# One hybrid decoder block on one core: no remainders on GpSimd, row tiles by token halves, another order of the products of the merge, and accumulating transfers

## The chip, the core and the metric

The kernel runs on one NeuronCore of a Trainium2 chip. The core has a matrix engine (TensorE, PE in the profile; PEld is its loading of weights), a vector engine (VectorE, DVE), an activation engine (ScalarE, ACT), a programmable vector engine (GpSimd, POOL) and an engine that issues most transfers (SyncE, SP). Each works through its own queue in order and waits on semaphores. Matrix products land in PSUM, eight banks of 128 partitions by 512 floats; everything else works on SBUF, 128 partitions wide. The metric is the device time of one execution in microseconds. The kernel before takes 2135.2 us, the median of three runs (2126.42 to 2137.53).

## The reference

One layer, batch 1, 1024 tokens, model width 1024, all in float32. What is computed:

```
h      = rms_norm(x, norm_mix_g) * (1 + scale) + shift        # scale, shift, gate from c @ w_ada
proj   = h @ w_in                                             # q, k, v of two mixers, gates
ya     = rms_norm(diff_attention(q1, q2, k1, k2, v))          # 8 heads, causal, 128 wide values
ym     = sigmoid(mo) * rms_norm(mlstm_chunkwise(q, k, v))     # 4 heads, 256 wide
merged = sigmoid(ga) * (ya @ w_a) + sigmoid(gm) * (ym @ w_m)
x      = x + gate * (merged @ w_out)
x      = x + gate' * (relu(h' @ w_ff1)^2 @ w_ff2)             # h' from x as h above
```

The change touches the way operands are split (everywhere), the product ya @ w_a with the merge behind it, the product merged @ w_out, and the first groups of w_ff1.

## The kernel before

**Split operands.** PE multiplies in a reduced format (F32R). Every float32 operand v is split into a high part (a copy on ACT into F32R) and a remainder v - high (a subtraction), and a product of two operands is three matmuls: high x high, high x remainder, remainder x high. The copy is line 319 in `parts` and line 152 in `load_w`; the subtraction is `split_lo`, line 138. `split_lo` and `parts` take an argument `pool`: True puts the subtraction on GpSimd, False on DVE, None lets a running count choose (`pick`, which charges GpSimd three units where DVE has one, or a plain alternation within `split_lo`). `add` (line 315) and `sub` (line 312) choose in the same way.

**Seven products instead of eight.** The large products are done in 2x2 blocks of 512 by the Strassen-Winograd scheme: sums of blocks are formed on both sides, seven products are made, and sums of the products give the four output blocks. Class `Chunks` does it for ya @ w_a, for merged @ w_out and for w_ff2. `prep` forms the next product's operand sums (`operands`) and splits them, in two halves q; `run` issues a product, four blocks j of 12 matmuls each (line 327, tiles `cps`, `s_op`, `t_op`), and calls an `out` function after each block, `out_a` for w_a and `out_o` for w_out. The operand tiles exist twice (`self.s`, `self.t`), so that `prep` runs one product ahead, and its splits wait until the product two before has been read. The orders are `ORDER_X` = (1, 7, 2, 4, 5, 6, 3) for w_a (and w_ff2) and `ORDER_Y` = (1, 2, 5, 6, 3, 7, 4) for w_out. In `out_a`, product 6 adds into three tiles and merges two blocks.

**The merge.** `merge` takes a finished block of ya @ w_a, in PSUM or SBUF. It loads the same block of the other branch (`mb`, from mb_d in DRAM, line 1677) and of the gate (`sga_d`), makes tanh on ACT (line 1285), the gating (sg + 1) * block on DVE (line 1288) and the addition of mb on DVE (line 315). mb_d is written before by `m_unit` through transfers that GpSimd issues (line 1302).

**Stages.** After the norm and the first projections come the mLSTM heads, with the gate projections (`gate_unit`) woven in between; the attention heads, each with the next head's projection (`at_qk`); in the last head the reload of ym (`reload`) and the units of ym @ w_m; then w_a, w_out, and the feed-forward. Weights are loaded ahead by `plan`, whose entries call `load_w`. Before the feed-forward, `half0` and `right` form and split the row blocks of h' for the first four groups, on GpSimd or DVE as `pick` says.

**Row tiles.** `ActX` holds split rows for hT and later ym in four tiles of the pool `xp`, which has four slots. They are cut by halves of the features: tile [r][k // 4] holds all 1024 tokens of four of the eight feature blocks, for r = high or remainder. The tiles of the merge (`mg`) and one operand set of `Chunks` take the same four slots afterwards.

**Order of the work.** The program is written out as a sequence of calls. The framework then lists it for each engine by itself: it takes ready work in program order by its own estimates of durations, and an operation whose inputs are there early can be placed ahead of its place in the program.

Of the kernel before, what the change touches and what calls it, by code (L numbers as in the profile page):

```python
# [17 lines left out]
P = 128  # L18
# [18 lines left out]
def kernel(  # L37
# [131 lines left out]
    class ActX:  # L169


        def __init__(self, name):
            self.t = [[xp.tile([P, 4, S], F32R, name=f"{name}{r}{i}", tag="x") for i in range(2)] for r in range(2)]

        def at(self, k, t0, n):
            return tuple(self.t[r][k // 4][:, k % 4, t0:t0 + n] for r in range(2))
# [350 lines left out]
    def modulate(q):  # L527
# [15 lines left out]
        def step(n):  # L543
# [9 lines left out]
            hh, hl = (hT.t[r][q][:, k:k + 2, m * 256:(m + 1) * 256] for r in range(2))  # L553
# [205 lines left out]
    class Conv(Group):  # L759
# [9 lines left out]
        def out(self, t, hf, n, a, b, into):  # L769
            c = crow[t][:, hf * 512:hf * 512 + 512]  # L770
            if b is None:
                nc.scalar.activation(c, a, AF.Copy)
            else:
                add(c, a, b, None if (t, hf) == (1, 1) else False)
            if (t, hf) in ((0, 1), (1, 0)):
                behind.extend(self.conv(t))
# [25 lines left out]
    class Gate(Group):  # L802
# [9 lines left out]
        def out(self, t, hf, n, a, b, into):  # L812
# [5 lines left out]
            else:  # L818
                add(c, a, b, None if (t, hf) == (1, 1) else False)
# [39 lines left out]
    def ml_in(h, hd):  # L859


        def half(hf):
# [7 lines left out]
            for i in (1, 0):  # L870
                for t in range(2):
                    d = hd["qk"][i, t, hf] = wt("r", [P, 2, 512], "qk", F32R)
                    parts((d[:, 0, :], d[:, 1, :]), hd["kc"][t][:, ts_] if i else q[:, t, :])

        def vals(g):
# [7 lines left out]
            parts((vt[:, :, 0, 0:256], vt[:, :, 1, 0:256]), vr)  # L883
# [212 lines left out]
    def at_v(h, vts):  # L1096
# [3 lines left out]
        def read(g):  # L1100
# [3 lines left out]
            parts((vt[:, :, 0, :], vt[:, :, 1, :]), vr.rearrange("p t (a d) -> p (t a) d", a=2))  # L1104
# [212 lines left out]
    def gate_cols(i):  # L1317
        cols((C_GA, C_GM)[i // 4] + (i % 4) * 256, True)

    def qk_cols(h):  # L1320
# [3 lines left out]
        plan.append(lambda: load_w([(srcs[q], lambda v, q=q: v[:, :, q * P:(q + 1) * P]) for q in range(2)], KT, True))  # L1324
# [6 lines left out]
    for h in range(AH):  # L1331
        if h % 2 == 0 and h // 2 not in (0, 1, 2):
            cols(C_AV + h * P, True)
# [4 lines left out]
    for u in range(4):  # L1338
        plan.append(lambda u=u: load_cols(w_m[0], u * 256, True))
# [142 lines left out]
    for h in range(AH):  # L1482
# [18 lines left out]
    class Chunks:  # L1501
# [6 lines left out]
        def __init__(self, xs):  # L1508
            self.n, self.jobs, self.made, self.tmp = 0, [], 0, {}
# [15 lines left out]
        def add(self, order, left, right, out, sums=None):  # L1525
            self.jobs += [(i, order, left, right, out, sums) for i in order]
# [9 lines left out]
        def prep(self):  # L1536
# [5 lines left out]
            i, order, left, right, _, sums = self.jobs[n]  # L1542
            s, t = self.s[n % 2], self.t[n % 2]
            for q in range(2):
                l, r = self.operands(i, order[1] == 7, left, right, sums, q)
                self.split(s(q), l)
                self.split(t(q), r)

        def operands(self, i, x, left, right, sums, q):
            b11, b12, b21, b22 = (right.get((m, q)) for m in (11, 12, 21, 22))  # L1550
            if sums is None:
                a11, a12, a21, a22 = (left[m, q] for m in (11, 12, 21, 22))
            two = range(2)

            def tmp(tag, name):
                return [wt(tag, [P, 512], name) for _ in two]
# [4 lines left out]
            r = {1: b11, 2: b21, 3: b22, 4: b21, 5: b12, 6: b11, 7: b12}[i]  # L1561
            if x:
                if i == 7:
                    r = tmp("f", "t3")
                    for k in two:
# [5 lines left out]
            elif i == 5:  # L1571
                r = self.tmp["r", q] = tmp("f", "t1")
                for k in two:
                    sub(r[k], b12[:, k], b11[:, k], False)
            elif i == 6:
                minus(b12, b22, b12)
                for k, v in enumerate(self.tmp["r", q]):
                    sub(b11[:, k], b22[:, k], v, False)
            elif i == 4:
                minus(b21, b21, b11)  # L1580
            if sums is not None:
                return sums(i, q), r
            l = {1: a11, 2: a12, 3: a12, 4: a22, 5: a21, 6: a11, 7: a21}[i]
            if i == 3:
                minus(a12, a12, a11)
            elif x:
                if i == 7:
                    l = tmp("m", "s3")
                    for k in two:
                        sub(l[k], a11[:, k], a21[:, k], False)  # L1590
                elif i == 5:
                    add(a21, a21, a22, False, 2)
                elif i == 6:
                    minus(a11, a21, a11)
            elif i == 5:
                l = self.tmp["l", q] = tmp("m", "s1")
                for k in two:
                    add(l[k], a21[:, k], a22[:, k], False)
            elif i == 6:
                minus(a21, a11, a21)  # L1600
                for k, v in enumerate(self.tmp["l", q]):
                    sub(a11[:, k], v, a11[:, k], False)
            return l, r

        def run(self):

            i, order, _, _, out, _ = self.jobs[self.n]
# [21 lines left out]
    ORDER_Y = (1, 2, 5, 6, 3, 7, 4)  # L1629
# [44 lines left out]
    def merge(dst, c, f0, t0):  # L1674

        mb = wt("m", [P, 512], "mb")
        nc.sync.dma_start(mb, mb_d[f0:f0 + P, t0:t0 + 512])
        sg = gated(sga_d, f0, t0)(c)
        busy(1)
        add(dst, sg, mb, False)  # L1680

    def out_a(i, j, ps):
        f0, f1 = j * P, 512 + j * P
        if i == 1:
            nc.scalar.activation(u1[:, j], ps, AF.Copy)
        elif i == 7:
            nc.scalar.activation(m22[:, j], ps, AF.Copy)
        elif i == 2:
            merge(m11[:, j], ps, f0, 0)
        elif i == 4:  # L1690
            add(m12[:, j], ps, u1[:, j], False)
        elif i == 5:
            add(m22[:, j], ps, m22[:, j], False)
            add(m22[:, j], m22[:, j], u1[:, j], False)
        elif i == 6:
# [384 lines left out]
```

## Time and profile before

| | before |
|---|---|
| median of three runs | 2135.2 us (2126.42 to 2137.53) |
| the profiled execution's own time | 2137.04 us |
| its span, first to last instruction | 2135.2 us |
| busy: PE, DVE, ACT, POOL | 2001.3, 1660.5, 1045.5, 234.0 us |
| granted PE clock over the span | 0.97 |
| POOL's subtractions of 128x1024 | 36, 2453 ns each |
| transfers on the queue of POOL | 9.44 MB, against 285.35 MB on SP's |

Busy time is the union of an engine's instructions; the idle time of an engine is put down to what ended it, by semaphore. A row of a group reads: line, engine, operation, output and input tiles, shapes, count, then busy time and mean duration in ns, then the idle time of the engine before them and its releasers. A row of a timeline reads: start, length, engine, line, operation, tiles, shape, count, and in brackets the idle time just before. Where operations of DVE follow each other closely, the recorded durations overlap by some 0.08 us, so their spacing is shorter than their duration.

### The profile page before, as it was taken

How to read it: one execution, taken by the hardware profiler on the slowest of the kernel's cores; microseconds unless marked ns; L12 is line 12 of the kernel's file. 1: busy time of each engine (PE TensorE's matmuls, PEld its weight loads, DVE VectorE, ACT ScalarE, POOL GpSimd, SP SyncE). 2: the span in 40 equal slices, each digit the busy share in tenths (PEclk: the TensorE clock that was granted, in tenths of full speed). 3: DMA queues.
4: the chain of work that ended last, by engine and by line, in shares of the span. 5: the costliest groups of instructions: out<-in, count | busy, mean ns of one | idle time of the engine just before them, and what ended most of it. 6: DMA issues, size and time to landing. Idle time of an engine off the chain costs nothing. (4 is left out here: it accounts for less than half of the span.)

```text
span 2135.2 us, 30324 instructions
## 1 busy us (share of the span) xinstructions
PE 2001.3 (94%) x11201; PEld 1732.3 (81%) x11201; DVE 1660.5 (78%) x2887; ACT 1045.5 (49%) x1966; POOL 234.0 (11%) x251
## 2 busy tenths in 40 slices
PE   5889999999889999999999999888799999899999
PEld 5889898888778899898988788677678888788887
DVE  7876668987765468989877747998777667898896
ACT  5522234444565557777756634435444555433332
POOL 0000000002232211111112410004400000000000
PEclk7999999999999999999999999999899999999999
DMA  8354453235655342222222665503344445845432
GB/s 284 111 163 156 150 162 118 91 107 193 192 177 162 107 122 60 80 60 80 60 66 69 202 222 169 171 1 123 114 169 156 153 148 201 305 139 167 150 117 80
DMA packets 210634, 296.72 MB, mean 139 GB/s; under 512 B 14067, under 2 KB 132494, under 8 KB 210486
## 3 DMA queue, kind: packets, MB, share of 16 engines
q1 hardware_dynamic: 207542, 285.35, 41.8%
q0 software_dynamic: 2944, 9.44, 1.2%
q8 instruction: 88, 1.44, 0.3%
q14 instruction: 60, 0.49, 0.1%
HBM read 206.43 MB, written 79.93 MB: 134 GB/s over the span
## 5 line engine op out<-in xcount | busy, mean ns | idle before, releaser
L327 PE MATMUL cps<-t_op,s_op 128*128 128x512 f32 x2016 | 478.4, 398 | 27.3 <-ACT s_op L319 10.9
L327 PEld LDWEIGHTS cps<-t_op,s_op 128*128 128x128 f32 x2016 | 383.1, 191 | 119.6 <-ACT s_op L319 12.6
L319 ACT ACTIVATE w_op<-w_st 128x512 fp32r<-128x512 f32 (+1 forms) x192 | 130.6, 695 | 183.8 <-PE pb L327 57.8
L138 DVE TENSOR_TENSOR w_op<-w_st,w_op 128x512 fp32r<-128x512 f32 (+1 forms) x192 | 146.7, 784 | 6.3 <-ACT w_op L319 4.1
L165 PE MATMUL ps<-w_hi,hT 128*128 128x256 f32 x512 | 146.9, 287 | 0.0
L166 PE MATMUL ps<-w_lo,hT 128*128 128x256 f32 x512 | 146.7, 286 | 0.0
L167 PE MATMUL ps<-w_hi,hT 128*128 128x256 f32 x512 | 146.2, 286 | 0.0
L319 ACT ACTIVATE s_op<-act 128x1024 fp32r<-128x1024 f32 x56 | 58.4, 1051 | 142.9 <-PE cps L327 108.0
L138 POOL TENSOR_TENSOR w_lo<-w_st,w_hi 128x1024 fp32r<-128x1024 f32 x36 | 87.9, 2453 | 313.3 <-ACT w_hi L152 310.0
L1198 ACT ACTIVATE ee<-ee,mneg 128x256 f32<-128x256 f32 (+7 forms) x128 | 98.4, 770 | 21.0 <-DVE mneg L1194 20.6
L327 PE MATMUL pa<-b,w_op 128*128 128x512 f32 x384 | 96.4, 402 | 6.7 <-ACT m L430 6.6
L1188 PE MATMUL lg<-kb,qe 128*128 128x512 f32 (+3 forms) x384 | 96.1, 361 | 4.2 <-DVE kb L1160 1.9
L327 PE MATMUL pc<-bt,w_op 128*128 128x512 f32 x384 | 96.1, 396 | 3.8 <-DVE w_op L138 2.0
L166 PEld LDWEIGHTS ps<-w_lo,hT 128*128 128x128 f32 x512 | 98.0, 191 | 1.5 <-issue 0.9
L165 PEld LDWEIGHTS ps<-w_hi,hT 128*128 128x128 f32 x512 | 97.9, 191 | 0.8
L167 PEld LDWEIGHTS ps<-w_hi,hT 128*128 128x128 f32 x512 | 98.0, 191 | 0.2
L327 PEld LDWEIGHTS pa<-b,w_op 128*128 128x128 f32 x384 | 74.1, 194 | 23.1 <-ACT m L430 7.6
L327 PEld LDWEIGHTS pc<-bt,w_op 128*128 128x128 f32 x384 | 71.1, 188 | 24.6 <-DVE w_op L138 7.0
L315 DVE TENSOR_TENSOR acc<-cps,acc 128x512 f32<-128x512 f32 x116 | 76.9, 684 | 13.0 <-PE cps L327 12.8
L715 DVE SCALAR_TENSOR_TENSOR ac<-crow,cond,ac 128x256 f32<-128x256 f32 x112 | 54.0, 482 | 34.2 <-DMA crow<-in_w_ada_dram 32.5
L1194 DVE CUSTOM_DVE_ANT_0 ee<-lg,bs 128x512 f32<-128x512 f32 (+4 forms) x128 | 70.1, 559 | 12.4 <-PE lg L1188 11.4
L138 DVE TENSOR_TENSOR s_op<-act,s_op 128x1024 fp32r<-128x1024 f32 x56 | 68.2, 1219 | 5.4 <-ACT s_op L319 5.3
(418 smaller groups left out, 4948.8 us busy)
## 6 DMA issues: line engine op xcount, KB each, us to landing
w_st<-in_w_in_dram SPq DMA_DIRECT2D x72, 512.0 KB, 4.5
act<-act_d SPq DMA_DIRECT2D x56, 512.0 KB, 3.6
w_st<-in_w_ff_dram SPq DMA_DIRECT2D x36, 512.0 KB, 4.1
crow<-in_w_ada_dram SPq DMA_DIRECT2D x32, 512.0 KB, 3.9
w<-in_w_ff_dram SPq DMA_DIRECT2D x32, 512.0 KB, 5.0
act_d<-s SPq DMA_DIRECT2D x48, 256.0 KB, 2.0
wa<-in_w_ada_dram SPq DMA_DIRECT2D x16, 512.0 KB, 4.8
mq_d<-cv SPq DMA_DIRECT2D x16, 512.0 KB, 2.8
```

The lines of the kernel that those rows point to most:

```text
L138: return (nc.gpsimd if pool else nc.vector).tensor_tensor(dst, src, hi.bitcast(F32), op=ALU.subtract)
L165: nc.tensor.matmul(o, lhsT=ah, rhs=bh, start=first, stop=False)
L166: nc.tensor.matmul(o, lhsT=ah, rhs=bl, start=False, stop=False)
L167: nc.tensor.matmul(o, lhsT=al, rhs=bh, start=False, stop=last)
L315: (nc.gpsimd if pick(pool, n) else nc.vector).tensor_tensor(o, a, b, op=ALU.add)
L319: nc.scalar.activation(dst[0], src, AF.Copy)
L327: nc.tensor.matmul(ps, lhsT=p, rhs=q, start=first and k == 0 and r == 0, stop=k == 3 and r == 2, skip_group_check=True,)
L715: nc.vector.scalar_tensor_tensor(ac, stv[:, k, :], cond[:, kk:kk + 1], ac, op0=ALU.mult, op1=ALU.add)
L1188: nc.tensor.matmul(lg[:, 0:max(256, w)], lhsT=hd["q"][hf][e][:, r, q4 * P:(q4 + 1) * P], rhs=hd["k"][e][:, c0:c0 + max(256, w)], start=r = ...
L1194: nc.vector.tensor_tensor_reduce(ee[:, c0:c0 + w], lg[:, 0:w], hd["bs"][:, n - c0 - w:n - c0][:, ::-1], -0.125, first, ALU.add, ALU.min, last,
L1198: nc.scalar.activation(ee[:, 0:n], ee[:, 0:n], AF.Exp, bias=mneg[:, e:e + 1], scale=-1.0, accum_out=ssum[:, e:e + 1])
```

## The change

1. Every remainder and every block sum that was on GpSimd, or could be by `pick`, goes to DVE: `parts(..., False)`, `sub(..., False)`, and False in the weight loads of `plan` and in `reload`. GpSimd keeps the powers of the norms, masks, memsets and its transfers.
2. `ActX` is cut by halves of the tokens: tile [t0 // 512][r] holds all eight feature blocks of 512 tokens.
3. In `Chunks.operands`, products 6 and 7 without given sums use another form of the scheme: product 6 forms all operand sums, half of them (`rest`) behind its own splits, and product 7 takes a22 minus the changed a11. The orders are `ORDER_Y` = (1, 2, 6, 7, 4, 5, 3) for w_a and `ORDER_Z` = (1, 2, 6, 5, 3, 7, 4) for w_out. w_ff2 keeps `ORDER_X`. `out_a` and `out_o` follow: product 6 now adds into one tile. w_out's weights are loaded in the order 11, 21, 12, 22.
4. `merge` gates into the destination itself, and a transfer issued by GpSimd adds mb_d's block to it in SBUF (`accum_op=ALU.add`).

```diff
-            self.t = [[xp.tile([P, 4, S], F32R, name=f"{name}{r}{i}", tag="x") for i in range(2)] for r in range(2)]
+            self.t = [[xp.tile([P, KT, 512], F32R, name=f"{name}{r}{i}", tag="x") for r in range(2)] for i in range(2)]
...
-                    parts((d[:, 0, :], d[:, 1, :]), hd["kc"][t][:, ts_] if i else q[:, t, :])
+                    parts((d[:, 0, :], d[:, 1, :]), hd["kc"][t][:, ts_] if i else q[:, t, :], False)
...
-        cols((C_GA, C_GM)[i // 4] + (i % 4) * 256, True)
+        cols((C_GA, C_GM)[i // 4] + (i % 4) * 256, False)
...
-        plan.append(lambda u=u: load_cols(w_m[0], u * 256, True))
+        plan.append(lambda u=u: load_cols(w_m[0], u * 256, False))
...
-            filler += reload(ym, ym_d, True) + units[0:12 * 2]
+            filler += reload(ym, ym_d, False) + units[0:12 * 2]
...
+            l = {1: a11, 2: a12, 3: a12, 4: a22, 5: a21, 6: a11, 7: a11}[i]
+            r = {1: b11, 2: b21, 3: b22, 4: b21, 5: b12, 7: b11}.get(i)
+            behind = ()
+            if i == 6:
+                add(a21, a21, a22, False, 2)
+                minus(a11, a21, a11)
+                minus(b12, b12, b11)
+                r = [wt("f", [P, 512], "t2") for _ in range(2)]
+                for k in range(2):
+                    sub(r[k], b22[:, k], b12[:, k], False)
+                def rest():
+                    for k in range(2):
+                        sub(b21[:, k], b21[:, k], r[k], False)
+                        sub(b11[:, k], r[k], b11[:, k], False)
+                    minus(a12, a12, a11)
+                behind = (rest,)
+            elif i == 7:
+                minus(a11, a22, a11)
...
-    ORDER_Y = (1, 2, 5, 6, 3, 7, 4)
+    ORDER_Y = (1, 2, 6, 7, 4, 5, 3)
+    ORDER_Z = (1, 2, 6, 5, 3, 7, 4)
...
-        mb = wt("m", [P, 512], "mb")
-        nc.sync.dma_start(mb, mb_d[f0:f0 + P, t0:t0 + 512])
-        sg = gated(sga_d, f0, t0)(c)
-        busy(1)
-        add(dst, sg, mb, False)
+        sg = wt("f", [P, 512], "sg")
+        nc.sync.dma_start(sg, sga_d[f0:f0 + P, t0:t0 + 512])
+        nc.scalar.activation(sg, sg, AF.Tanh, scale=0.5)
+        nc.vector.scalar_tensor_tensor(dst, sg, 1.0, c, op0=ALU.add, op1=ALU.mult)
+        nc.gpsimd.dma_start(dst, mb_d[f0:f0 + P, t0:t0 + 512], accum_op=ALU.add)
...
         elif i == 4:
             add(m12[:, j], ps, u1[:, j], False)
+            merge(m12[:, j], m12[:, j], f1, 0)
         elif i == 5:
             add(m22[:, j], ps, m22[:, j], False)
             add(m22[:, j], m22[:, j], u1[:, j], False)
-        elif i == 6:
-            add(m12[:, j], ps, m12[:, j], False)
-            add(m22[:, j], ps, m22[:, j], False)
-            add(u1[:, j], ps, u1[:, j], False)
-            merge(m12[:, j], m12[:, j], f1, 0)
             merge(m22[:, j], m22[:, j], f1, 512)
...
-            wo = pieces("e", "wo", w_out[0], False, (11, 12), behind)
+            wo = pieces("e", "wo", w_out[0], False, (11,), behind)
...
+                elif i == 6:
+                    add(u2[:, j], ps, u2[:, j], False)
                 elif i == 5:
-                    add(hi[:, c1], ps, hi[:, c1], False)
-                    for q in (lo[:, c1], hi[:, c0], hi[:, c1]):
-                        add(q, q, u2[:, j], False)
-                elif i == 6:
-                    for q in (lo[:, c1], hi[:, c0], hi[:, c1]):
-                        add(q, ps, q, False)
+                    nc.scalar.activation(u1[:, j], ps, AF.Copy)
...
-        parts(B[1 + k // 4](k % 4), e_at(k))
+        parts(B[1 + k // 4](k % 4), e_at(k), False)
...
-            sub(b22, b22, b12)
+            sub(b22, b22, b12, False)
...
-        parts(B[i](k), src)
+        parts(B[i](k), src, False)
```

More of the change, by code (lines that the diff above doesn't have):

```diff
@@ L773, in out @@
             else:
-                add(c, a, b, None if (t, hf) == (1, 1) else False)
+                add(c, a, b, False)
             if (t, hf) in ((0, 1), (1, 0)):
@@ L818, in out @@
             else:
-                add(c, a, b, None if (t, hf) == (1, 1) else False)
+                add(c, a, b, False)
             f0 = self.f + t * P
@@ L1525, in add @@
         def add(self, order, left, right, out, sums=None):
-            self.jobs += [(i, order, left, right, out, sums) for i in order]
+            self.jobs += [(i, left, right, out, sums) for i in order]
         def split(self, dst, src):
@@ L1541, in prep, with operands @@
             self.made += 1
-            i, order, left, right, _, sums = self.jobs[n]
+            i, left, right, _, sums = self.jobs[n]
             s, t = self.s[n % 2], self.t[n % 2]
             for q in range(2):
-                l, r = self.operands(i, order[1] == 7, left, right, sums, q)
+                l, r, behind = self.operands(i, left, right, sums, q)
                 self.split(s(q), l)
                 self.split(t(q), r)
-        def operands(self, i, x, left, right, sums, q):
+                run(behind)
+        def operands(self, i, left, right, sums, q):
             b11, b12, b21, b22 = (right.get((m, q)) for m in (11, 12, 21, 22))
[L1551 to L1556, printed above, removed]
             def minus(o, a, b):
                 sub(o, a, b, False, 2)
-            r = {1: b11, 2: b21, 3: b22, 4: b21, 5: b12, 6: b11, 7: b12}[i]
-            if x:
+            if sums is not None:
+                r = {1: b11, 2: b21, 3: b22, 4: b21, 5: b12, 6: b11, 7: b12}[i]
                 if i == 7:
-                    r = tmp("f", "t3")
-                    for k in two:
+                    r = [wt("f", [P, 512], "t3") for _ in range(2)]
+                    for k in range(2):
                         sub(r[k], b22[:, k], b12[:, k], False)
@@ L1603, in operands @@
-            return l, r
+                return sums(i, q), r, ()
+            a11, a12, a21, a22 = (left[m, q] for m in (11, 12, 21, 22))
+            l = {1: a11, 2: a12, 3: a12, 4: a22, 5: a21, 6: a11, 7: a11}[i]
[9 more added lines that the diff above has]
+                def rest():
+                    for k in range(2):
+                        sub(b21[:, k], b21[:, k], r[k], False)
[4 more added lines that the diff above has]
+                minus(a11, a22, a11)
@@ L1605, in run @@
+            return l, r, behind
         def run(self):
-            i, order, _, _, out, _ = self.jobs[self.n]
+            i, _, _, out, _ = self.jobs[self.n]
             s, t = self.s[self.n % 2], self.t[self.n % 2]
@@ L1770 @@
             }
[L1771 removed]
+            ch.add(ORDER_Z, mgs_of, wo, out_o)
     NG = DFF // 256
```

72 lines of the change are left out of this document (24 added, 48 removed).

## The prediction

> **What bounds the kernel now.** I read the page's engine totals first, then busy time by stretch, then what TensorE (PE) waited for, then the timeline at those waits. The page:
>
> ```profile
> PE 2001.3 (94%) x11201; PEld 1732.3 (81%) x11201; DVE 1660.5 (78%) x2887; ACT 1045.5 (49%) x1966; POOL 234.0 (11%) x251
> ```
>
> PE is the bound; only its 134 us of idle time, and its slow clock, can be won. The stretches that the change touches, and the rest behind them, cut by stage (columns: stretch, its length, busy time and count for PE, weight loads, DVE, ACT and POOL, granted clock, DMA share, GB/s): mLSTM, attention, remaining w_m units, w_a product, w_out product, first feed-forward groups, rest.
>
> ```profile
> 533.80:785.00 251.20, 230.97 (x1433) 205.93 (x1432) 151.74 (x374) 138.45 (x326) 70.21 (x121) 0.95 0.51 154
> 785.00:1168.00 383.00, 361.98 (x2745) 343.60 (x2743) 325.19 (x857) 268.66 (x671) 53.50 (x37) 0.99 0.24 68
> 1168.00:1288.80 120.80, 114.84 (x560) 93.94 (x560) 77.48 (x150) 57.42 (x124) 38.95 (x36) 0.97 0.60 201
> 1288.80:1378.10 89.30, 78.89 (x339) 63.28 (x337) 75.33 (x93) 43.11 (x56) 0.54 (x1) 0.96 0.61 195
> 1378.10:1478.10 100.00, 89.03 (x367) 70.37 (x368) 94.47 (x129) 42.24 (x71) 11.45 (x9) 0.92 0.13 46
> 1478.10:1566.50 88.40, 73.24 (x311) 58.00 (x309) 65.51 (x86) 43.93 (x78) 38.00 (x26) 0.92 0.41 138
> 1566.50:2135.20 568.70, 557.86 (x2410) 452.09 (x2410) 454.10 (x591) 236.11 (x328) 0.00 (x0) 1.00 0.48 161
> ```
>
> The three stretches from 1288.8 to 1566.5 idle PE for 36.5 us (10.4, 11.0, 15.2) and hold its lowest clocks; in the w_out product DVE is busy 94.5 of 100 us. There DVE feeds PE late. PE's waits in these three, the longest, and then the spot at 1365 us:
>
> ```profile
> PE cps L327 <- DVE t_op L138: 6.7, 2, 6.1
> PE pa L327 <- ACT m L430: 6.6, 1, 6.6
> ...
> PE cps L327 <- DVE xr L315: 4.4, 1, 4.4
> PE tp L1785 <- DVE rw L1790: 4.4, 1, 4.4
> ```
>
> ```profile
> 1365.05 1.88 DVE L315 TENSOR_TENSOR mg<-cps,mg 128x512 f32<-128x512 f32 x3
> 1366.85 1.28 DVE L1288 SCALAR_TENSOR_TENSOR sg<-sg,mg 128x512 f32<-128x512 f32 x2
> 1368.05 1.29 DVE L315 TENSOR_TENSOR mg<-sg,mb 128x512 f32<-128x512 f32 x2
> ...
> 1371.28 0.77 PE L327 MATMUL cps<-t_op,s_op 128*128 128x512 f32 x1 [3.66 <-DVE mg L315]
> ...
> 1378.14 0.80 PE L327 MATMUL cps<-t_op,s_op 128*128 128x512 f32 x1 [6.09 <-DVE t_op L138]
> 1389.75 1.22 DVE L138 TENSOR_TENSOR s_op<-mg,s_op 128x1024 fp32r<-128x1024 f32 x1
> 1390.88 1.22 DVE L138 TENSOR_TENSOR t_op<-wo,t_op 128x1024 fp32r<-128x1024 f32 x1
> ```
>
> Old product 6 hands DVE seven operations per block j (three adds, two gatings, two adds of mb), 1365.05 to 1369.26 = 4.2 us a block, 16.8 us for four, and the operands of the next chunk queue behind. From the same rows: back to back, a 512-wide operation costs 0.6 us (4.2/7), a 1024-wide one 1.13 us (1389.75 to 1390.88).
>
> **A long gap costs twice.**
>
> ```profile
> 1515.58 5.49 PE pa L327 x12
> 1569.94 2.72 PE pb L327 x12
> 1843.10 76.58 PE cps L327 x330
> ```
>
> Behind the 6.6 us gap twelve matmuls take 5.49 us instead of 2.72: 2.8 us more. The third row gives PE's full rate, 76.58/330 = 0.232 us, so a product of 48 matmuls takes 11.1 us. The Trainium skill (TensorE: Matmul & The Clock Gate, What's actually happening) says that PE halves its clock after an idle window of about 3.4 us; the trace agrees with the halving, and by the rule a stall that shrinks below 3.4 us would lose its clock penalty entirely.
>
> **GpSimd holds DVE up.** In attention:
>
> ```profile
> 870.53 4.78 POOL L138 TENSOR_TENSOR w_lo<-w_st,w_hi 128x1024 fp32r<-128x1024 f32 x2 [6.07 <-ACT w_hi L152]
> ...
> 873.55 1.79 DVE L271 SCALAR_TENSOR_TENSOR nt<-nt 128x16 f32<-128x16 f32 x1
> 875.88 0.16 DVE L272 SCALAR_TENSOR_TENSOR rr<-nt,rr 128x16 f32<-128x16 f32 x1
> 877.58 0.63 PE L1151 MATMUL tp<-ksq,raw 128*128 128x128 f32 x4 [2.26 <-DVE raw L1142]
> ```
>
> A 16-element operation takes 1.79 us while POOL works, its like 0.16 us after it; PE then waits 2.26 us.
>
> **The change, part by part.**
>
> (1) Remainders off GpSimd. The two largest groups of POOL, over the whole span:
>
> ```profile
> L138 POOL TENSOR_TENSOR w_lo<-w_st,w_hi 128x1024 fp32r<-128x1024 f32 x36 | 87.9, 2453 | 313.3 <-ACT w_hi L152 310.0 <-PE tp L950 3.1
> L138 POOL TENSOR_TENSOR ym<-w_st,ym 128x512 fp32r<-128x512 f32 x16 | 21.3, 1350 | 22.8 <-ACT ym L1276 22.8
> ```
>
> 36 wide splits go to DVE at 1.13 us, 41 us over the kernel; the narrow ones (16 in the second row, more in the feed-forward head below) at 0.6 instead of 1.35. Against it stand the hold-ups that end. In attention (785 to 1168 us):
>
> ```profile
> L271 DVE SCALAR_TENSOR_TENSOR nt<-nt 128x16 f32<-128x16 f32 x14 | 11.0, 785 | 0.2
> L270 DVE TENSOR_TENSOR nt<-rr 128x16 f32<-128x16 f32 x15 | 10.6, 707 | 0.1
> ```
>
> Against 0.16 us free, these give back 14x0.62 + 15x0.55 = 17 us. Moved in: two wide splits a head plus the w_av pair and the first w_m units, some 18x1.13 = 20 us. DVE (325 of 383 us) thus does not change in sum, but its short links no longer wait 1.6 us. What PE waited for from mLSTM into attention:
>
> ```profile
> PE tp L1151 <- DVE raw L1142: 11.4, 6, 2.4
> PE num L167 <- DVE sw L929: 8.5, 6, 2.4
> PE num L165 <- ACT sw L928: 5.8, 6, 2.1
> ```
>
> The upper bound is these 25.7 us; below zero it reaches if the inserted 1.13 us splits stand in the same chains. I take -3 us in attention (bounds -11 to +8) and -4 in mLSTM (-14 to +5), where DVE has room (152 of 251 us); -1 (-3 to +2) in the w_m stretch, 77 of 121 us. The work that hides the splits is the next heads' matmuls; without that cover each costs its 1.13 us.
>
> In the first feed-forward groups POOL is busy 38 us, DVE 65.5, in one chain:
>
> ```profile
> 1505.95 1.78 DVE L315 TENSOR_TENSOR w_st<-w_st 128x512 f32<-128x512 f32 x1
> 1511.38 0.68 DVE L312 TENSOR_TENSOR w_st<-w_st 128x512 f32<-128x512 f32 x1
> ```
>
> The same operation takes 1.78 beside POOL, 0.68 without. Of POOL's 26 operations one is a row-norm power and stays; 25x0.6 = 15 us go to DVE, and about ten such hold-ups of 1.1 us end. DVE: 65.5 + 15 - 11 = 70 us, less than PE's 73, and the chain no longer alternates. The 6.6 and 4.4 us waits sit in it, with 2.8 us of slow clock. I take -8; bounds -2 (DVE at 70 of 80 still feeds late) and -15 (all idle time of the stretch). The Trainium skill (SBUF — State Buffer, Who interferes with whom) calls this an exclusive lock between GpSimd reads and DVE operations with two SBUF inputs; by it all 38 us of POOL stand serially against DVE, so the move would free 38 - 15 = 23 us of DVE time where my rows give 11.
>
> (2) Order of the products. Out operations on DVE, w_a: per block 7 adds and 4 merges of two = 15 before, 5 adds and 4 gatings = 9 after; times four blocks 24 fewer, 14 us. Adds in w_out: 11 per block before, 9 after, 8 fewer, 5 us; ACT gets four copies. Operand sums: eight 512-wide and four 1024-wide per half before in w_out, six and five after: 9.3 and 9.3 us, nothing; in w_a likewise. What moves is the peak: no product now gives DVE more than three operations a block (7.2 us against 11.1 us of PE). Old product 6's 16.8 us and its 9.8 us of PE wait go. But new product 6, third in each order, needs all sums at once. In w_out, counted from the end of the last w_a product: the last block's add and gating 1.2, splits of the second product 4.5 (their buffers free only then), first half's sums 4.6, its split 2.3, rest 3.5, second half's 4.6 and 2.3 = 23.0 us, against two products 22.3 us; with up to 5 us of backlog PE stalls 1 to 6 us. I take 4. In w_a the sums can run beside the w_m units, 0 to 2; I take 1; and 2 around the row norms (the 4.4 us wait). Stretch 1288.8 to 1478.1 now: 189.3 us; at full rate 14x11.1 + 3 us of transposes = 158.4; lost 31, left 7: -24. Bounds: -12 (half the stalls come back elsewhere) and -31.
>
> (3) Accumulating transfers. 16 loads of mb leave SP's queue, 16 adds leave DVE (counted above), POOL issues 16 transfers. No accumulating one is in the trace; nearest rows:
>
> ```profile
> ya_d<-ya POOLq DMA_DIRECT2D x16, 256.0 KB, 2.3
> mb_d<-sg POOLq DMA_DIRECT2D x16, 256.0 KB, 3.3
> mb<-mb_d SPq DMA_DIRECT2D x16, 256.0 KB, 4.1
> vr<-mv_d SPq DMA_DIRECT2D x8, 512.0 KB, 7.2
> ```
>
> 2.3 us as a plain store, 7.2 us as if twice the bytes moved; I take 4.1, the same bytes from the same tensor. m11, m12 and m22 are gated a product or more before use. m21's last block is gated 1.2 us after the last product and needed at 5.7: at 4.1 hidden, at 7.2 it adds 2.7 us to the stall. Each transfer waits on POOL for its gating; behind it stand only further transfers and two row-norm powers, which come later.
>
> (4) Row tiles by token halves: same bytes, same matmuls. Matmuls now start while other parts of a tile are still unwritten, so regions are tracked, and I take 0; ym's first half may load some us earlier (-2), or a slot come free later (+2).
>
> **Sum**: 24 + 8 + 3 + 4 + 1 = 40 us, against the profiled execution's own 2137.0 us (span 2135.2 plus 1.8 around): 2097. The median of three, 2135.2, lies 1.8 lower, so 2095 as a median; I say 2096.
>
> **Rivals.**
> A, deeper: every GpSimd hold-up was on the path and w_out's third product doesn't stall. 31 + 15 + 11 + 8 = 65: about 2070. For: the 2.3 us waits repeat at every head. Against: the splits need DVE time there. The Trainium skill's lock rule would make it this way. Chance 0.15.
> B, partial: moved splits stretch the softmax chains. A third of 20 + 20 us exposed, +14, and the 8 us of (1) before 1288.8 not won: 2096 + 22 = 2118. For: DVE there is 85% busy. Chance 0.17.
> C, accumulation slow: at 20 us a transfer the third w_out product waits 15 us more: 2111. It decides from 4.5 us. Against: every 256 KB row lies at 2.3 to 4.1. Chance 0.05.
> D, no change: DVE stays the limit, (2) wins 12, attention and mLSTM lose 8 and 5: 2137 - 12 - 2 + 13, about 2136. Chance 0.12.
> E, slower: an in-order split on DVE stands waiting for ACT's w_hi. On POOL this wait blocked nobody:
>
> ```profile
> L138 POOL TENSOR_TENSOR w_lo<-w_st,w_hi 128x1024 fp32r<-128x1024 f32 x26 | 62.9, 2429 | 86.6 <-ACT w_hi L152 83.4 <-PE tp L950 3.1
> ```
>
> 83.4/26 = 3.2 us each; if DVE stood so long, 2096 + 83 = 2179. It decides from 40/26 = 1.5 us a split. Against: the split goes into DVE's order when w_hi is expected, and DVE follows ACT everywhere else with little idle time. Chance 0.06.
>
> **How the numbers follow.** The forecast (2084 to 2110) keeps 0.45. A measurement of this kernel tells 0.5%, 10.7 us: faster is A, B, C and the forecast, 0.82; same D, 0.12; slower E, 0.06. The range takes in A and B, 2068 to 2126, and leaves out D, E and the tail of A.
>
> **What would show it.** Right: PE idle in the three stretches down from 36.5 to about 15 us, clock near 0.97; no hold-ups of DVE's 128x16 operations above 0.3 us; old product 6's queue of seven gone; one stall of 1 to 6 us at the third w_out product. Wrong: DVE idle with w_hi as its releaser in attention (E), PE waiting on mg behind a transfer (C), or PE idle unchanged from 1288.8 to 1566.5 (D).

## The result and the profile after

The changed kernel takes 2080.7 us (median of four runs, 2076.2 to 2082.6), the kernel before 2136.4 on the same chip: a ratio of 0.9746, 95% interval 0.9713 to 0.978, or 55.6 us less. The forecast was 2096 us, with a range of 2068 to 2126. The sign held and the time lies in the range, but the gain was 1.4 times the forecast of 40 us, and it does not lie where the sum put it.

The page of the profiled execution after (own time 2082.6 us, span 2080.8), its line of busy times:

```profile
PE 1990.2 (96%) x11201; PEld 1723.6 (83%) x11201; DVE 1645.0 (79%) x2948; ACT 1044.6 (50%) x1966; POOL 71.9 (3%) x170
```

POOL's 162 us of work are gone, and DVE, which took its subtractions over, is busy 15 us *less*. Part of that is work which the new orders and the accumulating transfers take from DVE: with the splits alone (the first experiment below) DVE is busy 1665.3 us, 5 more than before, for 97 more operations. Busy time by stage, cut at the same events in both kernels: mLSTM, attention, the remaining w_m units, the w_a product, the w_out product, and the feed-forward's head up to its 288th matmul. First before, then after (stretch, length, busy of PE, PEld, DVE, ACT, POOL, clock, DMA share, GB/s):

```profile
518.60:787.40 268.80, 246.62 (x1507) 218.55 (x1505) 163.40 (x388) 148.06 (x343) 79.30 (x125) 0.96 0.54 163
787.40:1233.50 446.10, 421.38 (x3036) 391.51 (x3037) 371.51 (x960) 307.19 (x760) 80.20 (x59) 0.98 0.29 85
1233.50:1289.00 55.50, 55.19 (x265) 45.96 (x265) 29.07 (x44) 17.78 (x32) 10.73 (x12) 1.00 0.62 216
1289.00:1371.30 82.30, 77.94 (x338) 62.86 (x336) 68.53 (x85) 38.01 (x50) 0.54 (x1) 1.00 0.60 191
1371.30:1478.30 107.00, 89.98 (x369) 70.78 (x370) 101.47 (x137) 47.34 (x78) 11.65 (x9) 0.89 0.17 59
1478.30:1569.80 91.50, 75.47 (x321) 59.84 (x321) 68.61 (x92) 46.12 (x82) 37.80 (x26) 0.93 0.42 143
```

```profile
516.50:772.00 255.50, 241.74 (x1511) 213.90 (x1510) 165.12 (x415) 147.90 (x343) 26.34 (x98) 0.99 0.57 171
772.00:1196.60 424.60, 417.44 (x3031) 389.01 (x3032) 367.51 (x995) 305.08 (x759) 13.08 (x23) 0.99 0.31 89
1196.60:1252.10 55.50, 55.12 (x266) 45.92 (x264) 33.80 (x47) 17.54 (x31) 5.42 (x9) 1.00 0.63 213
1252.10:1337.60 85.50, 79.61 (x338) 64.09 (x337) 62.11 (x73) 38.58 (x52) 11.39 (x14) 0.98 0.67 188
1337.60:1421.80 84.20, 82.09 (x370) 66.10 (x369) 82.66 (x112) 44.92 (x76) 5.79 (x6) 1.00 0.22 62
1421.80:1510.20 88.40, 77.32 (x322) 60.56 (x320) 75.51 (x125) 49.92 (x86) 1.76 (x2) 0.92 0.48 159
```

| stage | before | after | difference | forecast |
|---|---|---|---|---|
| mLSTM | 268.8 | 255.5 | -13.3 | -4 (-14 to +5) |
| attention | 446.1 | 424.6 | -21.5 | -3 (-11 to +8) |
| w_m units | 55.5 | 55.5 | 0 | -1 |
| w_a and w_out | 189.3 | 169.7 | -19.6 | -24 (-31 to -12) |
| feed-forward head | 91.5 | 88.4 | -3.1 | -8 (-15 to -2) |

The forecast's stretches were cut elsewhere (its attention ended at 1168 us, where its w_m stretch began), so its -3 and -1 stand together against the second and third rows. The differences make -57.5; the spans differ by 54.4. What lies ahead of mLSTM is 2.1 us shorter, and the last stage (w_ff2, code not touched) measured 322.3 us before and 327.5 after. Over all the profiles of this document, with the same code in that stage, it came out between 320.4 and 327.5 us. The two profiles of the kernel after have 327.5 and 326.9, so chance between executions is not shown to be the reason; why this stage differs is open.

In attention, small DVE operations of the row norms (`nt`) and of the softmax (`ssum`), and POOL's splits of weights (line, engine, operation, tiles, shape, count, busy us, mean ns), before:

```profile
L271 DVE SCALAR_TENSOR_TENSOR nt<-nt 128x16 f32<-128x16 f32 (+1 forms) x29 | 13.6, 470 | 0.3
L270 DVE TENSOR_TENSOR nt<-rr 128x16 f32<-128x16 f32 x14 | 10.1, 718 | 0.1
L1204 DVE SCALAR_TENSOR_TENSOR ssum<-ssum,nlam 128x1 f32<-128x1 f32 x63 | 23.2, 368 | 0.7
L138 POOL TENSOR_TENSOR w_lo<-w_st,w_hi 128x1024 fp32r<-128x1024 f32 x18 | 43.1, 2410 | 67.4 <-ACT w_hi L152 67.3
```

and after (line numbers are one or two higher):

```profile
L138 DVE TENSOR_TENSOR w_lo<-w_st,w_hi 128x1024 fp32r<-128x1024 f32 x18 | 21.9, 1215 | 4.9 <-ACT w_hi L152 4.8
L1206 DVE SCALAR_TENSOR_TENSOR ssum<-ssum,nlam 128x1 f32<-128x1 f32 x63 | 13.4, 215 | 0.4
L272 DVE SCALAR_TENSOR_TENSOR nt<-nt 128x4 f32<-128x4 f32 (+1 forms) x28 | 4.6, 165 | 0.3
L271 DVE TENSOR_TENSOR nt<-rr 128x16 f32<-128x16 f32 x14 | 2.3, 166 | 0.2 <-ACT rr L270 0.2
```

DVE took in 21.9 us of weight splits, and three rows alone gave back 13.6 - 4.6 + 10.1 - 2.3 + 23.2 - 13.4 = 26.6 us. It also took in 12.3 us of narrow splits (`ym` and `va`), and still its busy time in attention fell by 4.0 us, so other operations became shorter too. PE's 11.4 us of waits for `raw` are no longer in the view of waits. PE's waits from the w_a product to the end of the head, after, the three largest:

```profile
PE pc L328 <- ACT w_op L320: 5.1, 2, 3.7
PE cps L328 <- DVE mg L316: 4.3, 1, 4.3
PE tp L1778 <- DVE xr L1729: 2.0, 1, 2.0
```

### The profile page after: what moved, and what is told of

It reads as the page before. It is cut to its first block, busy times and chain, and to the rows that moved or that the text cites. A ratio compares the mean times of both kernels' runs of the same rounds, so it can differ in the third digit from the quotient of the medians.

```text
span 2080.8 us, 30233 instructions
## 1 busy us (share of the span) xinstructions
PE 1990.2 (96%) x11201; PEld 1723.6 (83%) x11201; DVE 1645.0 (79%) x2948; ACT 1044.6 (50%) x1966; POOL 71.9 (3%) x170
## 4 chain that ended last, share of the span: by engine, by line
PE 63%; DVE 12%; DMA 11%; issue 8%; ACT 4%; POOL 1%; SPq 0%; POOLq 0%; DVEq 0%; ACTq 0%
PE cps L328 16%; PE pb L328 8%; PE pc L328 7%; PE pa L328 7%; PE pd L328 4%; DMA crow<-in_w_ada_dram 4%; PE ps L166 3%; PE ps L165 3%; PE ps L167 3%; PE lg L1190 3%; PE pv L1243 3%; DVE ac L717 2%; DMA ex<-ea_d 1%; PE tp L1223 1%; PE ops L579 1%
## 5 line engine op out<-in xcount | busy, mean ns | idle before, releaser
L138 DVE TENSOR_TENSOR w_op<-w_st,w_op 128x512 fp32r<-128x512 f32 (+1 forms) x192 | 144.3, 770 | 10.9 <-ACT w_op L320 8.9
L1190 PEld LDWEIGHTS lg<-kb,qe 128*128 128x128 f32 x384 | 61.7, 193 | 11.5 <-DVE mneg L1196 6.7
```

The lines of the kernel that those rows point to most:

```text
L138: return (nc.gpsimd if pool else nc.vector).tensor_tensor(dst, src, hi.bitcast(F32), op=ALU.subtract)
L1190: nc.tensor.matmul(lg[:, 0:max(256, w)], lhsT=hd["q"][hf][e][:, r, q4 * P:(q4 + 1) * P], rhs=hd["k"][e][:, c0:c0 + max(256, w)], start=r = ...
```

## The experiments

Two theories stood at the start. **Company**: in mLSTM and attention GpSimd's reading held DVE up, and this was on the path. **Small part**: the splits are worth what the forecast said, and the rest of the gain belongs to the orders or the token halves. Where a run is compared with the kernel after, that is 2080.7 us or, run again in the last group, 2082.4.

**One part each: the splits, the orders.** In the first, the kernel before with `False` at each place where the change puts it for a split or a sum that GpSimd had:

```diff
-        cols((C_GA, C_GM)[i // 4] + (i % 4) * 256, True)
+        cols((C_GA, C_GM)[i // 4] + (i % 4) * 256, False)
...
-        parts(B[i](k), src)
+        parts(B[i](k), src, False)
```

> The kernel before with one part of the change alone: every remainder, sum and split that GpSimd had (weights, query and key, values, merge's reload, first feed-forward operands) goes to VectorE; token halves, product orders and the accumulation stay as before. Theory 1 (in the mLSTM and attention stages VectorE's small operations, held up while GpSimd works beside them, and GpSimd's own slow remainders, were on the path): those two stages lose the 13 and 21.6 us that the whole change took out of them, the feed-forward's head a few more, so 2095 to 2103 us, with the products' stretch still near 189 us. Theory 2 (the prediction's sizes were right for this part, -3, -4 and up to -8, and the rest of the gain belongs to the token halves or to the orders): 2120 to 2126 us.

Measured: 2101.4 us (2097.5 to 2102.4), ratio 0.9839 (0.9817 to 0.9862): 33.2 us less. The time is in the first theory's range, but not by the stages it named: mLSTM lost 14.6 us (254.2), attention 14.8 and not 21.6, the head 11.3.

In the second, the kernel after with all of that, the token halves and the accumulation taken back, so that the new orders stand alone:

> The kernel after with all but merge's product orders taken back: feature halves, remainders on GpSimd, the other branch's blocks loaded and added by VectorE. Theory 1 (parts add up): the two stretches of merge's products get shorter by 17 to 24 us and nothing else moves, so 2112 to 2119 us; mLSTM and attention keep their times of before, 268.8 and 446.1 us. Theory 2 (the new orders pay only with GpSimd out of the way): the stretch gets shorter by under 6 us, so above 2130 us.

Measured: 2112.4 us (2111.1 to 2113.5), ratio 0.9894 (0.9873 to 0.9915): 22.2 us less, in the first theory's range: w_a and w_out together take 167.3 us, 22.0 less. mLSTM, which should not move, takes 272.6. Attention, w_a, w_out and the head by stage, the splits alone:

```profile
774.50:1205.80 431.30, 418.59 (x3032) 389.18 (x3033) 368.33 (x995) 305.87 (x759) 13.08 (x23) 0.99 0.30 88
...
1262.40:1344.50 82.10, 77.97 (x338) 62.87 (x337) 68.63 (x85) 37.96 (x50) 0.54 (x1) 1.00 0.59 193
1344.50:1450.90 106.40, 89.34 (x369) 70.01 (x370) 101.77 (x143) 47.47 (x78) 3.98 (x3) 0.89 0.17 58
1450.90:1531.10 80.20, 73.48 (x321) 58.93 (x320) 71.28 (x118) 47.48 (x82) 1.07 (x1) 0.96 0.48 164
```

and the orders alone:

```profile
788.60:1233.80 445.20, 420.10 (x3037) 390.15 (x3038) 370.81 (x960) 307.19 (x760) 80.20 (x59) 0.99 0.29 85
...
1289.40:1366.90 77.50, 77.50 (x338) 63.08 (x337) 69.32 (x85) 40.26 (x53) 0.54 (x1) 1.00 0.63 207
1366.90:1456.70 89.80, 85.20 (x370) 67.91 (x369) 87.34 (x115) 45.32 (x76) 9.44 (x7) 0.96 0.13 47
1456.70:1545.90 89.20, 75.56 (x320) 59.76 (x320) 78.82 (x109) 48.00 (x84) 21.84 (x15) 0.94 0.45 152
```

The gain before the merge comes from the splits: attention drops by 14.8 us with them, by 0.9 without. The two times add up (33.2 + 22.2 = 55.4), but the stages do not. Merge and head together take 280.8 us before, 268.7 with the splits, 256.5 with the orders, and 258.1 with both, where 244.4 would be the sum of the two gains. The difference is in the head: 80.2 us with the splits and the old orders, 85.6 to 89.2 in every run with the new ones but the last. In the old w_out stretch PE stood idle, and DVE did some of the head's work there: with the splits alone, four splits of the head's weights (`w_op`) and two scalings of `xr` lie in the w_out stretch that lie in the head after, where DVE is busy 75.5 us instead of 71.3. That is 4.2 us of work on DVE; how it makes 5 to 9 us of time was not traced. That the totals agree all the same is partly chance: the whole change gains 6.7 us more in attention than the splits alone (see the run with feature halves), and the profiled execution of the splits alone, 2097.5 us, was the fastest of its four.

**The weights' remainders back on GpSimd**, nothing else:

```diff
-        cols((C_GA, C_GM)[i // 4] + (i % 4) * 256, False)
+        cols((C_GA, C_GM)[i // 4] + (i % 4) * 256, True)
...
-        plan.append(lambda u=u: load_cols(w_m[0], u * 256, False))
+        plan.append(lambda u=u: load_cols(w_m[0], u * 256, True))
```

> The kernel after with only the weights' remainders of mLSTM, attention and w_m back on GpSimd (gates, query and key, values, w_m: some 34 operations 128x1024 of 2.4 us each); query, key, value and reload splits stay on VectorE. Theory 1 (GpSimd working beside VectorE is what costs, and these are 34 of 52 us of its split work in mLSTM and 43 of 67 us in attention): two thirds of 13 plus 21.6 us come back, so 2099 to 2107 us. Rival (what cost was the lateness of the splits that the core itself waits for, query, key and values, not the company): 2081 to 2088 us.

Measured: 2112.2 us (2108.9 to 2116.0), 30 to 31 us more than after, above the first range. With these 36 operations on GpSimd, 18 of them in attention, attention takes 446.8 us, as long as before, although the token halves and the other splits on DVE stay. mLSTM has 263.7 us, above the 254.2 to 260.8 of the ten runs in which GpSimd neither makes these remainders nor adds beside them. In attention PE waits for `raw` again:

```profile
PE tp L1153 <- DVE raw L1144: 7.3, 4, 2.3
```

**Company alone.** Three runs take this further. Beside each of those splits, which stay on DVE, GpSimd works on a scratch tile that nobody reads (`beside` is set where the run before had `True`):

```diff
+            if beside:
+                gp = wp.tile([P, 256], F32, name="gp", tag="gp", bufs=1)
+                for c in range(0, 1024, 256):
+                    nc.gpsimd.tensor_tensor(gp, st[:, c:c + 256], st[:, c:c + 256], op=ALU.add)
-            split_lo(lv, sv, hv, pool)
+            split_lo(lv, sv, hv, False if beside else pool)
```

> The kernel after with company only: each of the weights' remainders that the run with the weights back gave to GpSimd (gates, query and key, values, w_m) stays on VectorE, and GpSimd adds the loaded weights to themselves into a scratch tile beside it, four operations 128x256 a time; nobody waits for the result but the slot of the load. Nothing is left out. Theory 1 (VectorE is held up while GpSimd reads on-chip memory beside it, and that alone is the price): most of the 31 us that the run with the weights back lost, so 2100 to 2112 us, and VectorE's small operations are held up by 1 us and more again. Theory 2 (the price is the slow remainder itself, which the weights' users or the load's slot wait for): 2081 to 2088 us.

Measured: 2093.9 us (2087.8 to 2101.3), 11 to 13 more than after, with runs that do not overlap, and between the two ranges. Then fills in place of the adds:

```diff
-                for c in range(0, 1024, 256):
-                    nc.gpsimd.tensor_tensor(gp, st[:, c:c + 256], st[:, c:c + 256], op=ALU.add)
+                for _ in range(7):
+                    nc.gpsimd.memset(gp, 0.0)
```

> As the run in which GpSimd adds the weights to themselves, but GpSimd only fills the scratch tile, seven operations 128x256 a time, about as long by the 128x128 fills of 0.20 us: it writes and reads nothing. Theory 1a (it is GpSimd's reading that holds VectorE up): 2080 to 2085 us. Theory 1b (any work on GpSimd holds it up): near the run with the adds, 2100 us and more.

Measured: 2089.3 us (2087.3 to 2091.8). The run missed its question. The fills wait for nothing, so GpSimd did them all in the first 104 us, among and ahead of its powers for the first row norms; the first groups start at 83 instead of 75 us, which is as much as the whole loss. So the fills were tied to the loads by one small read:

```diff
-                for _ in range(7):
-                    nc.gpsimd.memset(gp, 0.0)
+                nc.gpsimd.tensor_tensor(gp[:, 0:2], st[:, 0:2], st[:, 0:2], op=ALU.add)
+                for _ in range(5):
+                    nc.gpsimd.memset(gp, 0.0)
```

> As the run in which GpSimd adds weights to themselves, but of each group of four adds only a first one of 128x2 reads the load, so that it waits for it, and five fills of 128x256 follow, 0.33 us each: GpSimd is as long at work at the same places and hardly reads. (In the run with fills alone nothing tied them to the loads, and they all ran in the first 104 us.) Theory 1a (GpSimd's reading is what holds VectorE up): mLSTM and attention at 256 to 258 and 424 to 426 us, the kernel within 2 us of after. Theory 1b (any work on GpSimd does): 262 and 434 us, the kernel 8 to 14 us slower than after.

Measured: 2080.0 us (2076.1 to 2089.3), the same as after. Attention as a stretch, with the weights back, then with the adds, then with the tied fills:

```profile
780.30:1227.10 446.80, 422.49 (x3037) 394.97 (x3038) 369.14 (x978) 307.25 (x760) 55.96 (x41) 0.97 0.29 84
```

```profile
778.10:1211.90 433.80, 421.63 (x3031) 390.45 (x3032) 376.12 (x995) 305.10 (x759) 70.81 (x103) 0.98 0.30 87
```

```profile
775.00:1200.00 425.00, 417.43 (x3032) 389.05 (x3033) 367.66 (x995) 305.39 (x759) 51.41 (x143) 0.99 0.30 89
```

GpSimd's largest group in it, and one of the norms' operations on DVE, in the same three runs (in the first also an operation of the same size with one input):

```profile
L138 POOL TENSOR_TENSOR w_lo<-w_st,w_hi 128x1024 fp32r<-128x1024 f32 x18 | 42.9, 2397 | 77.6 <-ACT w_hi L152 77.6
L271 DVE TENSOR_TENSOR nt<-rr 128x16 f32<-128x16 f32 x14 | 7.2, 514 | 0.2
L268 DVE TENSOR_SCALAR nt<-rr 128x16 f32<-128x16 f32 x14 | 2.4, 169 | 0.1
```

```profile
L157 POOL TENSOR_TENSOR gp<-w_st 128x256 f32<-128x256 f32 x80 | 57.9, 723 | 195.0 <-DMA w_st<-in_w_in_dram 151.3 <-DMA w_st<-in_w_m_dram 38.8
L276 DVE TENSOR_TENSOR nt<-rr 128x16 f32<-128x16 f32 x14 | 2.7, 194 | 0.2 <-ACT rr L275 0.2
```

```profile
L158 POOL MEMSET gp<- 128x256 f32 x100 | 31.3, 313 | 5.6
L277 DVE TENSOR_TENSOR nt<-rr 128x16 f32<-128x16 f32 x14 | 2.3, 166 | 0.2 <-ACT rr L276 0.2
```

With the tied fills GpSimd is busy 38 us more than after in attention, 31 of them fills and 7 the small reads, and this costs nothing (425.0 us). With the adds it is busy 58 us more, all reading, and this costs 9 us, though nobody uses the result. DVE's own work shows it, 376.1 us in the second stretch against 367.7 in the third for the same operations. The slot of the load, which must wait for the adds, is not what differs: in both runs SyncE's waits for it, from 500 to 1260 us, end with DVE's split, 93.2 us with the adds and 90.5 with the tied fills. So GpSimd's reads hold DVE up, its occupation does not. The Trainium skill (SBUF — State Buffer, Who interferes with whom) says so: a DVE instruction with two SBUF inputs contends with a GpSimd instruction that reads SBUF, not with one that only writes it; these runs agree, and so does the pair of rows of the first run, 514 ns with two inputs (TENSOR_TENSOR) and 169 with one (TENSOR_SCALAR). Not settled is how the other 13 us in attention (446.8 against 433.8) divide. A real remainder is one operation of 2.4 us where the adds are four of 0.72, and a small DVE operation stands behind a longer one (514 against 194 ns in the rows); and its result is 1.2 us later than DVE's, for weights that PE uses. PE's waits for `raw` come back with the remainders alone; with the adds PE does not wait for it.

**Feature halves again**, in the kernel after:

```diff
-            self.t = [[xp.tile([P, KT, 512], F32R, name=f"{name}{r}{i}", tag="x") for r in range(2)] for i in range(2)]
+            self.t = [[xp.tile([P, 4, S], F32R, name=f"{name}{r}{i}", tag="x") for i in range(2)] for r in range(2)]
```

> The kernel after with the row tiles cut by feature halves again. The splits alone took 14.9 us out of attention, the whole change 21.6. Theory 1 (token halves pay those 6 us in attention, where values of one half no longer wait for the whole tile): 2085 to 2089 us, attention near 431 us. Theory 2 (they cost and bring nothing, the difference is scatter between executions): 2078 to 2083 us.

Measured: 2087.3 us (2083.0 to 2087.7), 5 to 7 more than after. Attention is where it lies:

```profile
777.30:1207.00 429.70, 417.76 (x3031) 388.33 (x3032) 368.44 (x995) 305.67 (x759) 13.03 (x23) 0.99 0.30 88
```

The two runs with feature halves and DVE splits have 429.7 and 431.3 us; the eight with token halves and no such reading on GpSimd have 424.2 to 425.6. Token halves are worth some 5 us, in attention. With feature halves PE waits there twice for a remainder of `ym`, 2.0 us, a wait that is gone with token halves; the rest was not traced.

**The first feed-forward groups back on GpSimd or DVE by count:**

```diff
-            sub(src, b22, b12, False)
+            sub(src, b22, b12)
...
-        parts(B[i](k), src, False)
+        parts(B[i](k), src)
```

> The kernel after with the first feed-forward groups' right-hand sums and remainders on the planner's choice of engine again. Theory 1 (the groups' head, 13 us shorter at 96 matmuls but with 10 us given back later, gains 3 us net from this): 2083 to 2087 us. Rival (VectorE alone is what gives the 10 us back, GpSimd was help): 2073 to 2078 us. Theory 3 (GpSimd's part in the head is on the path as in attention): 2088 to 2096 us.

Measured: 2084.2 us (2081.5 to 2088.7), 2 to 3.5 more than after with overlapping runs, and the head at 89.1 us (88.4 after): with the new orders this part of the change is worth nothing that can be told.

**The accumulation undone:**

```diff
-        nc.gpsimd.dma_start(dst, mb_d[f0:f0 + P, t0:t0 + 512], accum_op=ALU.add)
+        mb = wt("m", [P, 512], "mb")
+        nc.sync.dma_start(mb, mb_d[f0:f0 + P, t0:t0 + 512])
+        add(dst, dst, mb, False)
```

> The kernel after with the accumulating transfers undone: the other branch's block is loaded into a row tile and VectorE adds it, 16 times. Theory 1 (the accumulation is hidden, as is the add): 2079 to 2084 us. Rival (an accumulating transfer that lands late holds up the w_out products, so taking it away gains): 2070 to 2077 us. Second rival (the adds stand ahead of splits in VectorE's queue, so the accumulation was worth something): 2085 to 2095 us.

Measured: 2078.1 us (2074.0 to 2082.4), just under the first theory's range: no difference that can be told. By stage there is one, and it cancels: w_out takes 89.6 us instead of 84.2, with DVE busy 87.9 instead of 82.7, but w_a 77.7 instead of 85.5, where PE has no idle time instead of 5.9 us, 4.3 of them one stall before the last product, and the clock is 1.00 instead of 0.98. That stall was the last question, beside the head's.

**The gates' slots, the head's weights, and after again.** One run has the gates in slots of their own:

```diff
-        sg = wt("f", [P, 512], "sg")
+        sg = wt("m", [P, 512], "sg")
```

and another also prepares the third and fourth group's weights earlier:

```diff
         g.weights((4,))
+    g2.load()
+    g2.weights((7, 5))
     run([g0.p4, g1.p4])
...
-            g.weights((7, 5, 6, 3, 4))
-            run([g.p7, g.p5, g.p6, g.p3, g.p4])
+            g.weights((6, 3, 4))
+            run([g.p7, g.p5])
+            if g is g2:
+                g3.load()
+                g3.weights((7, 5))
+            run([g.p6, g.p3, g.p4])
```

> The kernel after, unchanged, beside the next three: 2078 to 2083 us; it is the yardstick for differences of a few us.

> The kernel after with merge's gates loaded into the four row-tile slots that no longer hold the other branch's blocks, instead of the five that they share with sums. Theory (the first stretch of merge's products is 8 us longer, 85.5 against 77.5 us in the two runs without the accumulation, because a gate's load stands 6.5 us on SyncE for such a slot and the loads of w_out and VectorE's merge queue up behind it): that stretch comes down to 77 to 79 us and the kernel is 3 to 8 us faster than after, 2073 to 2078 us. Rival (the accumulating transfers themselves make it longer): the stretch stays at 85 us and the time within 2 us of after.

> The gates' slots as in the run for them, and in the feed-forward's head the weights of products 7 and 5 of the third group are loaded and prepared before the products 4 of the first two, those of the fourth group before products 6, 3 and 4 of the third. Theory (the 10 us that the head gives back are product-7 weights queued on VectorE behind sums that wait for TensorE: gaps of 3.7, 1.4 and 1.0 us and a clock of 0.88 after them): 4 to 9 us less than with the slots alone, 2066 to 2073 us. Rival (VectorE has too much work there whatever the order): within 2 us of the slots alone.

Measured: after 2082.4 us (2079.4 to 2087.2), slots alone 2077.3 (2075.4 to 2086.2), slots and head 2073.2 (2071.6 to 2074.1), ratio to before 0.9706 (0.969 to 0.9723). SyncE's waits around the end of w_a, after:

```profile
SPq L1669 <- DVE mg L1671: 18.1, 7, 5.7
```

with the slots of their own, and without the accumulation:

```profile
SPq L1669 <- DVE mg L1671: 19.0, 7, 6.1
```

```profile
SPq L1669 <- DVE mg L1671: 7.2, 5, 2.5
```

The theory on the slots falls: the gates' loads wait just as long, the stretch is 83.8 us in this run and 79.1 in the next, whose program is the same up to there, and the times overlap with after. On DVE, after:

```profile
1316.42 1.23 DVE L1664 TENSOR_TENSOR wo<-wo,gta 128x1024 f32<-128x1024 f32 x1 [2.56 <-DMA wo<-in_w_out_dram]
1317.56 0.69 DVE L1671 SCALAR_TENSOR_TENSOR mg<-sg,mg 128x512 f32<-128x512 f32 x1
```

A gate's load waits on SP until DVE has used an older gate; that gating stands in DVE's queue behind a scaling of w_out, which waits for its own load; and the next loads of w_out stand on SP behind the gate's. Why this holds on longer with the accumulation than without stays open.

The theory on the head holds, at the lower end of its 4 to 9 us (4.1 less than the slots alone). The head after, then with the early weights:

```profile
1421.80:1510.20 88.40, 77.32 (x322) 60.56 (x320) 75.51 (x125) 49.92 (x86) 1.76 (x2) 0.92 0.48 159
```

```profile
1423.40:1504.50 81.10, 73.95 (x322) 58.90 (x321) 75.84 (x126) 49.50 (x87) 1.77 (x2) 0.96 0.50 163
```

DVE does the same work, 75.8 and 75.5 us, in 81.1 instead of 88.4 us (87.1 in after run again); PE's idle time falls from 11.1 to 7.2 us and its clock rises from 0.92 to 0.96. The kernel with both edits beats after by 7.5 to 9.3 us, with runs that do not overlap.

## Why the prediction was right and where it was wrong

**What bounds it**: right. The gain is idle time and clock: PE's idle time fell from 134 to 91 us, and its busy time, for the same matmuls, by 11 us.

**(1) Remainders off GpSimd**: sign right, size wrong. Two steps failed. First, "The upper bound is these 25.7 us": as attention's bound it had only the largest of PE's waits, 11.4 us for `raw`, and of these 11.4 the forecast kept 3. With the splits alone attention lost 14.8 us: the wait for `raw` is gone whole, PE's idle time fell from 446.1 - 421.4 = 24.7 to 12.7 us, and its busy time by another 2.8. (Token halves then bring the idle time to 7.2.) The bound also left the clock out, since by the prediction's reading a stall under 3.4 us costs none. In the kernel before one of the waits for `raw`, 2.40 us long, was followed by 3.4 us at half the clock (0.50 in the second row, a stretch with its length, busy times and clock):

```profile
1031.70 0.63 PE L1151 MATMUL tp<-ksq,raw 128*128 128x128 f32 x4 [2.40 <-DVE raw L1142]
1033.10:1036.50 3.40, 3.40 (x18) 3.40 (x17) 3.40 (x9) 2.46 (x7) 0.00 (x0) 0.50 0.52 159
```

So a stall shorter than that can cost twice too; of the six waits for `raw` this one did. Second, "these give back ... 17 us" against 20 moved in. On one side that counted two rows of held-up operations and left out the third above, `ssum` (63 operations, 368 to 215 ns); on the other it left out the narrow splits of `ym` (10.9 us). DVE came out 4 us lighter in attention, not equal. In mLSTM the forecast took -4 and bounded at -14; it was -13.3, and 8.0 to 14.6 less than before in the ten runs named above: the bound nearly held, the -4 was too small. For the head, "-8" is what the splits do with the old orders (-11.3 measured, and DVE at 71.3 us where the sum gave 70); with the new ones they do nothing there that can be told. The step that failed for the head is adding (1) and (2) as if independent: work that (2) drives out of w_out has to go somewhere.

**(2) Orders**: right in kind, a little over. -24 forecast, -19.6 measured; 11.3 us left over, not 7. The stall did not come where it was put. The third w_out product loses 1.3 us in two gaps, not 4. w_a, given 1 us (0 to 2) at its third product, idles 5.9 us, 4.3 of them before its last product, where PE waits for DVE's adds into `mg`, not for a transfer. The queue of seven operations is gone: w_out's length fell from 107.0 to 84.2 us, its clock rose from 0.89 to 1.00.

**(3) Accumulation**: right that it is hidden, wrong price. From issue to landing (lowest, median, highest), after:

```profile
DMA to landing us min/median/max: 4.1/6.2/8.8
```

The forecast took 4.1 and put the point from which it decides at 4.5. "Every 256 KB row lies at 2.3 to 4.1" was misread: such rows of the kernel before go up to 5.9. At 6.2 no product waited, because "needed at 5.7" does not hold for m21's last block. That block belongs to the second half of the operands; its transfer was issued at 1345.4 us, the last four took at most 6.3 us, and that half's sum starts at 1358.96 (the first half's at 1349.59):

```profile
1349.59 1.22 DVE L316 TENSOR_TENSOR mg<-mg,mg 128x1024 f32<-128x1024 f32 x1
1358.96 1.22 DVE L316 TENSOR_TENSOR mg<-mg,mg 128x1024 f32<-128x1024 f32 x1
```

**(4) Token halves**: "I take 0" with 2 either way; it was some 5 us, in attention.

**Rivals.** A was right in its mechanism, GpSimd's hold-ups on the path, and near in its time, but not in its terms: it gave the stages before the merge 19 us, measured 34.8, and the products and the head 46, measured 22.7. The forecast's own errors partly cancel, and that is luck: before the merge the gain was 27 us over it, in the products and the head 9 under it, and w_ff2 gave 5 back. B is out, attention became shorter and not longer. E is out: in attention DVE waited for `w_hi` 4.8 us over 18 splits, where E needed 1.5 us for each. C and D are out by time. Of the signs named, the idle time in the three stretches fell from 37.4 to 19.1 us by the cuts used here (about 15 forecast), the clock weighted over them is 0.97 as forecast, and hold-ups of the 128x16 operations are gone.

## What to carry to other kernels

Ask of an engine off the path not only whether it is late, but whom its reads hold up: compare the mean duration of the same small operation with and without it, over all rows, and bound the gain by the stage's whole idle time of PE and its slow clock, not by its largest wait. When a stage with idle time is compressed, look for work of a later stage that was done in that idle time; here it made the head 5 to 9 us longer, and starting two groups' weights earlier brought some 6 us of it back.

## What the runs showed of the hardware that was not expected

DVE, given 97 more operations (36 of them 128x1024 splits) by the splits alone, was busy only 5 us more in all (1665.3 against 1660.5), where by their recorded durations (1.22 us for a wide one, 0.68 for a narrow one) they come to an estimated 85 us. Fills on GpSimd (128x256, 0.31 us) beside DVE cost it nothing: its 128x16 operation took 166 ns beside them, as without. An accumulating transfer of 256 KB holds GpSimd longer than a plain store of the same size, 0.86 us (median) against 0.54 for the issue. It lands later than that store, but hardly later than the plain loads of the gates beside it:

```profile
mb_d<-sg POOLq DMA_DIRECT2D x16, 256.0 KB, 2.5
sg<-sga_d SPq DMA_DIRECT2D x16, 256.0 KB, 6.0
mg<-mb_d POOLq DMA_DIRECT2D x16, 256.0 KB, 6.2
```

And profiles of kernels with the same code in a stage differ there by up to 7 us (w_ff2, 320.4 to 327.5), while two profiles of one kernel, after and after again, agree to 1.7 us in each stage of the table and to 0.6 in w_ff2. A difference of a few us in one stage between single profiles tells little unless several runs with the same code agree, as they do in attention.
